# Queries, keys and gates of all four retention heads as one Strassen up stage, passed through HBM

## The chip, the cores and the metric

The kernel is one program on one core of a Trainium2 chip. The metric is the device time of one execution in microseconds (us). The engines are PE (TensorE, matrix products), DVE (VectorE), ACT (ScalarE), POOL (GpSimd) and SP (SyncE, which here only issues DMAs).

## The reference, cut to what matters

A trunk of two layers over 1040 tokens (16 learned ones and 1024 of the input), width 1024. Layer 0 has the "even" mixer (a gated linear recurrence beside latent attention), layer 1 the "odd" mixer (retention). Each mixer is followed by a squared-ReLU MLP of width 4096, and each sublayer ends in a layer norm.

```python
def _odd_mixer(x, pos, w_in, w_out):
    qk = RET_HEADS * RET_QK_DIM                      # 4 heads x 256
    p = x @ w_in
    q, k, v, g = jnp.split(p, [qk, 2 * qk, 2 * qk + RET_MIX], axis=-1)   # RET_MIX = 4 x 512
    q = _rope(q.reshape(B, T, RET_HEADS, RET_QK_DIM), pos)
    k = _rope(k.reshape(B, T, RET_HEADS, RET_QK_DIM), pos) * (RET_QK_DIM ** -0.5)
    ...
    _, o_r = lax.scan(body, s, (to_chunks(q), to_chunks(k), to_chunks(v)))   # retention
    ...
    o = (of * lax.rsqrt(jnp.mean(jnp.square(of), axis=-1, keepdims=True) + EPS)).astype(x.dtype)
    y = o.transpose(0, 2, 1, 3).reshape(B, T, RET_MIX)
    return (jax.nn.silu(g) * y) @ w_out
...
    h = _layernorm(DN_ALPHA * h + mix, ln_mix_g[l], ln_mix_b[l])
    f = jnp.square(jax.nn.relu(h @ mlp_w1[l])) @ mlp_w2[l]
    h = _layernorm(DN_ALPHA * h + f, ln_mlp_g[l], ln_mlp_b[l])
```

## The kernel before

Everything is held transposed: a matrix is 8 tiles of 128 features by the tokens. A number in fp32 is carried as two fp32r parts, hi and lo, which ACT (a cast, L306) and DVE (source minus hi, L353, L634 or L300) make. A product of two such tiles is three matmuls, hi·hi, hi·lo and lo·hi (L333 to L335, in `mm3` and `gemm`).

The SBUF is 50 slots of 128 x 1040 numbers and the PSUM eight banks, handed out in turn. `later` and `pump` run generators in the background of a loop, `queue`, `feed` and `need` do the same for fetching and splitting weights; `advance(pumps, feeds)` calls both. A scheduler then sets the order on each engine, and within an engine the order is kept: an instruction that waits holds all behind it.

The program runs in stages, with their rough place in the profiled execution:

- The even mixer, and its norm: 0 to 500 us.
- The MLP of layer 0, `smlp(0)`: 500 to 1204 us. Its **up** half (`up`, `products`, L768 to L770) is a Strassen scheme: x and the weights are cut into 2 x 2 blocks, seven products of sums take the place of eight. A unit `u` is two times two tiles of weights, 16 units in all; each unit goes over two token halves `q`, with 7 products x 4 tiles x 3 matmuls of 260 columns. ACT (L791) and DVE (L794) collect them out of PSUM, DVE squares (L798), and sums of the result go to HBM (`h_scratch`). The **down** half takes blocks of 4 or 2 such units (`BLOCKS[0] = [4, 4, 4, 2]`) through Strassen again, and the last 4 of the 32 tiles by plain products. The norm (`chunk`, `norm_chunk`) adds squares over features with fp32 matmuls of ones (L524, L558, L570) and here leaves x in SBUF as hi and lo.
- The odd mixer, 1204 to 1925 us, head by head: values `v` (`ret_values`: 8 token tiles x 8 tiles of features x 3 matmuls of 512 columns, then `ret_tail` for the last 16 tokens, L1461 to L1464); keys (`ret_rope`: two tiles in three spans of 348 and 346 columns, the rotation on DVE straight out of PSUM); `ret_turn` (k turned by PE, L1507); queries (two tiles in two spans of 512); for heads 1 to 3 the values stand here, between the turn and the state. Then `retain` (the state, the scores, the output, L1588 to L1590), then the gates (four tiles of 512 columns, Silu on ACT, L1370) with `ret_norm` among them. The gated output of heads 0 to 2 goes to `y_scratch` in HBM through POOL's queue.
- The out projection (end of `odd_mixer`, and `enter`): 1925 to 2120 us. `enter` is the way into a Strassen stage: four norm chunks, x to HBM, and the sums that the seven products need (`sums_of`, `make_x`).
- The MLP of layer 1: as layer 0's, with tokens in quarters of 256, blocks `[4, 4, 4]`, 8 plain tiles at the end and the output: 2120 to 2813 us.

## Time and profile before

| what | us |
|---|---|
| median of three runs | 2818.78 (2817.33 to 2821.24) |
| the profiled execution | 2815.4 |
| its span | 2813.6 |
| PE busy, in 19318 records | 2720.2 (97%) |
| DVE busy | 1741.3 (62%) |
| ACT busy | 1050.1 (37%) |
| POOL busy | 496.8 (18%) |

The span is the time between the first and the last instruction of the profile. An engine's busy time counts overlapping matmuls once. In a window the time that PE is not busy is time lost by the whole program, when PE is the engine that all stages stand on; the granted clock (PEclk, 1.00 is full speed) tells what is lost while it is busy.

### The profile page before, as it was taken

The numbers are of one execution on the slowest core, as the hardware profiler recorded it, in microseconds if no ns is written. First come the engines' busy times: TensorE is split into PE (matmuls) and PEld (weight loads), VectorE is DVE, ScalarE is ACT, GpSimd is POOL, SyncE is SP. The second block draws the span as 40 slices with busy tenths as digits, with TensorE's granted clock in tenths as the row PEclk, the third lists the DMA queues.
The fourth block names the chain that finished last, engine by engine and source line by source line (L and its number), as shares of the span: only waits on it lengthen the run. The fifth ranks groups of instructions, "written<-read, shape, count | busy, mean of one in ns | idle before, by whom it ended". The sixth has DMA issues, their size and how long they took to land. (4 is left out here: it accounts for less than half of the span.)

```text
span 2813.6 us, 46690 instructions
## 1 busy us (share of the span) xinstructions
PE 2720.2 (97%) x19318; PEld 2566.8 (91%) x19318; DVE 1741.3 (62%) x2748; ACT 1050.1 (37%) x1787; POOL 496.8 (18%) x532
## 2 busy tenths in 40 slices
PE   8999999999999999999999999999999999999997
PEld 8898899999999999878878888789999999999997
DVE  6678868755576778544534535354387655677754
ACT  3757744433343233332414224141145333433223
POOL 1024441456520000010000000010004644000010
PEclk9999999999999999999999999999999999999998
DMA  3220130344474235011301313043204444644311
GB/s 137 76 73 5 62 121 31 122 145 155 139 281 145 105 123 167 17 45 50 115 16 45 120 37 114 16 135 128 83 31 136 150 133 153 240 165 145 103 68 60
DMA packets 111941, 294.84 MB, mean 105 GB/s; under 512 B 10529, under 2 KB 46881, under 8 KB 111729
## 3 DMA queue, kind: packets, MB, share of 16 engines
q1 hardware_dynamic: 93168, 225.08, 23.5%
q0 software_dynamic: 17984, 64.65, 6.8%
q8 instruction: 151, 2.47, 0.4%
q10 hardware_dynamic: 576, 2.13, 0.2%
q14 instruction: 62, 0.50, 0.1%
HBM read 206.83 MB, written 81.80 MB: 103 GB/s over the span
## 5 line engine op out<-in xcount | busy, mean ns | idle before, releaser
L768 PE MATMUL p<-s,s 128*128 128x260 f32 (+1 forms) x3248 | 903.1, 284 | 23.3 <-DVE s L893 7.3
L769 PE MATMUL p<-s,s 128*128 128x260 f32 (+1 forms) x3248 | 909.9, 283 | 2.4 <-DVE s L634 2.2
L770 PE MATMUL p<-s,s 128*128 128x260 f32 (+1 forms) x3248 | 895.6, 282 | 5.0 <-DVE s L634 5.0
L333 PE MATMUL p<-s,s 128*128 128x256 f32 (+9 forms) x2614 | 854.7, 329 | 20.8 <-POOL s L381 7.3
L334 PE MATMUL p<-s,s 128*128 128x256 f32 (+9 forms) x2614 | 846.6, 324 | 4.6 <-DVE s L384 2.9
L335 PE MATMUL p<-s,s 128*128 128x256 f32 (+9 forms) x2614 | 843.1, 324 | 5.8 <-DVE s L300 5.8
L306 ACT CAST s<-s 128x1024 fp32r<-128x1024 f32 (+7 forms) x587 | 506.4, 888 | 840.2 <-PE p L770 119.4
L768 PEld LDWEIGHTS p<-s,s 128*128 128x128 f32 x3248 | 607.7, 189 | 30.4 <-ACT s L306 8.8
L769 PEld LDWEIGHTS p<-s,s 128*128 128x128 f32 x3248 | 614.6, 189 | 4.2 <-DVE s L634 3.8
L770 PEld LDWEIGHTS p<-s,s 128*128 128x128 f32 x3248 | 607.6, 189 | 5.7 <-DVE s L634 5.7
L333 PEld LDWEIGHTS p<-s,s 128*128 128x128 f32 (+3 forms) x2614 | 490.8, 188 | 63.5 <-ACT s L1199 10.1
L334 PEld LDWEIGHTS p<-s,s 128*128 128x128 f32 (+3 forms) x2614 | 491.8, 188 | 39.2 <-DVE s L384 3.9
L335 PEld LDWEIGHTS p<-s,s 128*128 128x128 f32 (+3 forms) x2614 | 491.1, 188 | 40.0 <-DVE s L300 6.5
L634 DVE TENSOR_TENSOR s<-s,s 128x1024 fp32r<-128x1024 f32 (+2 forms) x311 | 380.7, 1235 | 108.9 <-ACT s L306 102.9
L791 ACT COPY s<-p 128x260 f32<-128x260 f32 (+1 forms) x256 | 93.5, 373 | 237.5 <-PE p L770 217.3
L893 DVE TENSOR_TENSOR s<-s,p 128x260 f32<-128x260 f32 (+1 forms) x328 | 132.6, 418 | 74.5 <-PE p L770 71.9
L300 DVE TENSOR_TENSOR s<-s,s 128x1024 fp32r<-128x1024 f32 x97 | 118.0, 1224 | 77.8 <-ACT s L306 55.0
L798 DVE SCALAR_TENSOR_TENSOR s<-s 128x1040 f32<-128x1040 f32 (+1 forms) x64 | 83.6, 1306 | 42.1 <-ACT s L791 41.9
L794 DVE TENSOR_TENSOR s<-s,p 128x260 f32<-128x260 f32 (+1 forms) x192 | 78.2, 417 | 44.3 <-PE p L770 35.9
L806 POOL TENSOR_TENSOR s<-s 128x520 f32<-128x520 f32 (+1 forms) x52 | 78.4, 1509 | 133.5 <-DVE s L798 108.6
L1442 DVE TENSOR_TENSOR s<-p,s 128x512 fp32r<-128x512 f32 x32 | 22.0, 690 | 125.4 <-ACT s L1441 125.4
L536 POOL TENSOR_TENSOR s<-s 128x512 f32<-128x512 f32 (+1 forms) x6 | 7.8, 1297 | 479.2 <-DVE s L532 467.6
(212 smaller groups left out, 2611.4 us busy)
## 6 DMA issues: line engine op xcount, KB each, us to landing
s<-in_w SPq DMA_DIRECT2D x76, 512.0 KB, 3.9
s<-h_scratch SPq DMA_DIRECT2D x49, 520.0 KB, 5.9
s<-in_w2s SPq DMA_DIRECT2D x48, 512.0 KB, 4.4
s<-h_scratch SPq DMA_DIRECT2D x42, 512.0 KB, 6.2
h_scratch<-s POOLq DMA_DIRECT2D x28, 520.0 KB, 3.7
y_scratch<-s POOLq DMA_DIRECT2D x24, 512.0 KB, 10.2
s<-y_scratch POOLq DMA_DIRECT2D x24, 512.0 KB, 5.6
h_scratch<-s POOLq DMA_DIRECT2D x24, 512.0 KB, 4.2
```

The lines of the kernel that those rows point to most:

```text
L300: (self.nc.gpsimd if self.pool_lo else self.nc.vector).tensor_sub(lo[:, :n], s[:, :n], hi.f[:, :n])
L306: self.nc.scalar.copy(out, in_)
L333: self.nc.tensor.matmul(ps, wh, xh, start=(i == 0), stop=False)
L334: self.nc.tensor.matmul(ps, wh, xl, start=False, stop=False)
L335: self.nc.tensor.matmul(ps, wl, xh, start=False, stop=(stop and i == n - 1))
L634: (eng or self.nc.vector).tensor_sub(l.t, raw.t, h.f)
L768: nc.tensor.matmul(ps, wh[:, c], xh[:, k, :], start=(start and k == 0), stop=False, skip_group_check=skip)
L769: nc.tensor.matmul(ps, wh[:, c], xl[:, k, :], start=False, stop=False, skip_group_check=skip)
L770: nc.tensor.matmul(ps, wl[:, c], xh[:, k, :], start=False, stop=(k == nk - 1), skip_group_check=skip)
L791: nc.scalar.copy(h[:, {0: 0, 5: 1, 4: 3, 3: 2}[p], :], ps)
L798: nc.vector.scalar_tensor_tensor(h[:, :, :], h[:, :, :], 0.0, h[:, :, :], ALU.max, ALU.mult)
L893: nc.vector.tensor_add(d, d, ps)
```

## The change

The odd mixer's queries, keys and gates of all four heads (32 tiles of 128 output features, 1040 tokens) become a third Strassen up stage (`ODD`), run before the heads: unit 4h is head h's keys, 4h+1 its queries, 4h+2 and 4h+3 its gates. The rotation is done by DVE in SBUF on whole quarters (`rope`), the Silu by ACT, and the results are written by SP's queue to `p_scratch` in HBM, as fp32. The heads then have only the values' products: `ret_load` fetches k and q of a head and splits them, in the background of the values, and `ret_close` does the norm, fetches the gates, multiplies and splits, in the background of the next head's values. `ret_values` now goes through the weights outermost, over two groups of four banks.

For this, x has to come out of layer 0's MLP through `enter`, as at the other entries: blocks `[4, 4, 4]` and 8 plain tiles, the norm in four chunks, x to HBM (`x_odd`) and sums for the seven products. During the last unit of the up stage the eight tiles of x are fetched again and split (`rows`, `fetch_x`, `make_p`), and the values' first weights with them. The out projection takes the residual x from `x_odd` by DMA, where DVE added hi and lo.

```diff
...
-BLOCKS = [[4, 4, 4, 2], [4, 4, 4]]
+BLOCKS = [4, 4, 4]
+ODD = 2
...
-PV = 6
+PV = 2
...
         for h in range(RET):
-            v = [d["wv1"][4 * h + i] for i in range(4)]
-            u += v if h == 0 else []
...
+        self.pairs.append((len(u), len(u) + len(o)))
+        u += o + [d["wv1"][i] for i in range(16)]
...
+            if self.stage == ODD:
+                if u % 4 < 2:
+                    self.later(0, self.rope(h, tabs[i], [self.hd[2 * u + r][:, 2 * n * q:2 * n * q + 2 * n] for r in range(2)]))
+                    return
+                nc.scalar.activation(h[:, :, :], h[:, :, :], AF.Silu)
+                for r in range(2):
+                    nc.sync.dma_start(self.hd[2 * u + r][:, 2 * n * q:2 * n * q + 2 * n], h[:, 2 * r:2 * r + 2, :])
+                self.aside.append(h)
+                return
...
+            if s == 4 and self.stage == ODD:
+                for u, q in streams:
+                    if u % 4 < 2:
+                        t = self.slot(F32, (P, 2, 2 * n))
+                        src = self.d["ropeq"][u // 4] if u % 4 else self.d["ropek"]
+                        nc.sync.dma_start(t[:, :, :], src[:, :, 2 * n * q:2 * n * q + 2 * n].rearrange("c p t -> p c t"))
+                        tabs.append(t)
...
+        self.queue(("X", s))
+        if s:
+            self.queue(("p", s - 1))
+        if s == 6:
+            self.queue(("X", 7), ("p", 6), ("p", 7), *[("v", i) for i in range(4)])
...
         for u in range(2, 16):
-            self.queue(("w", u + 1))
-            self.up([(u, 0), (u, 1)], True, at=moves(0) if u == 15 else None, rates=(0, 4 if u == 15 else 1), nxt=True)
+            if more or u < 15:
+                self.queue(("w", u + 1))
+            self.up([(u, 0), (u, 1)], True, at=at if u == 15 else None, rates=(0 if more else 2, 4 if u == 15 else 1), nxt=more or u < 14)
...
+        rec, wr = [self.ops["r", i] for i in range(4)], []
+        self.queue(*[("R", i) for i in range(4, 8)])
...
+        ws, y = [self.weight(reserve=50) for _ in range(4)], [self.ops["r", i] for i in range(4, 8)]
...
-        for c in range(4):
-            def gemm(ps, m):
-                self.gemm(ps, ws[m // 2], h, c * n, c * n + n, k0=4 * (m % 2))
...
-            tmp = self.chunk(c, gemm, True, rates=(5, 0))
...
-        return x, [t for ts in self.acc for t in ts]
+            self.enter(rec, wr, y, ws, self.g11, self.b11, out=self.out)
+        else:
+            self.layer(ODD)
+            self.enter(rec, wr, y, ws, self.g01, self.b01)
...
+        pr, xo = self.hd, self.xd
+        self.up_stage(self.rows)
+        x = []
+        for k in range(KT):
+            self.need("p", k)
+            x.append(self.ops["r", k])
...
+            kf, k, q = [], [], []
+            self.later(0, self.ret_load(pr, 8 * h, 0, T, k, kf))
+            self.later(0, self.ret_load(pr, 8 * h + 2, META, SEQ, q))
+            v = self.ret_values(x, h == 0)
+            if h == RET - 1:
+                for t in x:
+                    self.drop(*t)
+            self.settle()
             kt = self.ret_turn(h, kf)
-            cq, sq = self.slot(F32, (P, SEQ)), self.slot(F32, (P, SEQ))
-            nc.sync.dma_start(cq[:, :], d["ropeq"][h, 0])
-            nc.sync.dma_start(sq[:, :], d["ropeq"][h, 1])
...
-            if h:
-                v = self.ret_values(x)
             o = self.retain(h, q, k, v, kt)
...
-            for m in range(4):
...
-                    ps = self.bank("b")[:, :hi - lo]
-                    self.gemm(ps, w, x, META + lo, META + hi)
-                    silu = nc.scalar.activation(sg[m][:, lo:hi], ps, AF.Silu)
...
-                if m == NORM_AT:
-                    self.ret_norm(o, onesr)
...
+            self.later(0, self.ret_close(pr, h, o, ys))
+        y = self.reload(0) + self.reload(1)
...
-                nc.vector.tensor_add(self.acc[c][k // 4][:, k % 4, :], xh.f[:, cols], xl.f[:, cols])
...
+        self.acc = [self.x_chunk(c, xo, META) for c in range(4)]
...
             for c in range(4):
                 self.part(c, mp, lambda ps, m: self.gemm(ps, w[m % 2], y, c * n, c * n + n), True)
+                self.advance(6, 0)
             self.drop(*w[0], *w[1])
+            if mp == 1:
+                self.settle()
+                self.drop(aux, self.vc)
+                rec = self.reload(2)
...
+    def ret_load(self, pr, i, off, n, out, keep=None):
+        for j in range(2):
+            f = self.slot(F32, (P, n))
+            self.nc.sync.dma_start(f[:, :], pr[i + j][:, off:off + n])
+            yield True
+            h, l = self.slot(F32R, (P, n)), self.slot(F32R, (P, n))
+            self.split(f[:, :], h[:, :], l[:, :], h.f)
+            out.append((h, l))
+            if keep is None:
+                self.drop(f)
+            else:
+                keep.append(f)
+            yield True
+
+    def rope(self, h, tab, dst):
+        nc, n = self.nc, 2 * self.qn
+        t = self.slot(F32, (P, 2, n))
+        a, b = (h.t.rearrange("p (j r) n -> p j (r n)", j=2)[:, j, :] for j in range(2))
+        nc.vector.tensor_mul(t[:, :, :], a.unsqueeze(1).broadcast_to((P, 2, n)), tab[:, :, :])
+        yield True
+        nc.vector.tensor_mul(a, b, tab[:, 1, :])
+        yield True
+        nc.vector.tensor_mul(b, b, tab[:, 0, :])
+        yield True
+        nc.vector.tensor_sub(t[:, 0, :], t[:, 0, :], a)
+        yield True
+        nc.vector.tensor_add(t[:, 1, :], t[:, 1, :], b)
+        for r in range(2):
+            nc.sync.dma_start(dst[r], t[:, r, :])
+        self.drop(h, tab, t)
+        yield True
+
...
+    def ret_close(self, pr, h, o, ys):
...
+        yield from self.ret_norm(o)
+        for m in range(4):
+            g = self.slot(F32, (P, SEQ))
+            nc.sync.dma_start(g[:, :], pr[8 * h + 4 + m][:, META:])
+            nc.vector.tensor_mul(g[:, :], g[:, :], o[m][:, :])
+            self.drop(o[m])
+            yield True
+            yh, yl = self.slot(F32R, (P, SEQ)), self.slot(F32R, (P, SEQ))
+            self.split(g[:, :], yh[:, :], yl[:, :], yh.f)
...
+            if h < RET - 1:
+                for e, t in enumerate((yh, yl)):
+                    nc.gpsimd.dma_start(self.scratch[4 * h + m, e], t[:, :])
...
-        for i, (lo, hi) in enumerate(ATOK):
-            n = hi - lo
-            self.settle(hi)
...
-            self.pump(PV)
+        for group in (range(0, 4), range(4, 8)):
+            ps = [self.bank("all") for _ in group]
+            for u in range(4):
+                for i, t in zip(group, ps):
...
+                    for k in (2 * u, 2 * u + 1):
...
+                        nc.tensor.matmul(t, xh, wh, start=(k == 0), stop=False)
+                        nc.tensor.matmul(t, xh, wl, start=False, stop=False)
+                        nc.tensor.matmul(t, xl, wh, start=False, stop=(k == KT - 1))
...
+                    self.pump(PV)
+        self.ret_tail(x, ws, first)
...
+        if h < RET - 1:
+            self.ahead(4, 1, 1)
...
```

How the order on the engines moves is shown at three places. Names: `p_` is a PSUM tile, `s_` an SBUF slot, with a number of its own for each use; a row reads engine line, operation, out<-moving,stationary operand, shape.

**PE, from a head's turn of k to the products behind it.** Before, head 1: the last product of the keys, the turn (L1507), the queries' products (x is `s_1645`, `s_1646`).

```order
L335 MATMUL p_2179_17277<-s_1659_12684,s_2148_17039 128x346
L1507 MATMUL p_2184_17340<-consts_116,s_2161_17137 128x128
L1507 MATMUL p_2184_17340<-consts_116,s_2162_17138 128x128
L1507 MATMUL p_2185_17345<-consts_116,s_2161_17137 128x128
L1507 MATMUL p_2185_17345<-consts_116,s_2162_17138 128x128
L333 MATMUL p_2200_17380<-s_1645_12670,s_2163_17139 128x512
L334 MATMUL p_2200_17380<-s_1646_12671,s_2163_17139 128x512
```

After, head 1: the last product of the values' tail, then the turn (L1528; `s_2142` is the fetched k0, `s_2145` the fetched k1) and the scores of `retain` (`s_2149`, `s_2150` are hi and lo of q0, `s_2152`, `s_2153` of q1, `s_2143`, `s_2144` of k0, `s_2146`, `s_2147` of k1).

```order
L1508 MATMUL p_2158_17876<-s_2110_17552,s_2013_16885 48x512
L1528 MATMUL p_2162_17901<-consts_116,s_2142_17703 128x128
L1528 MATMUL p_2163_17906<-consts_116,s_2142_17703 128x128
L333 MATMUL p_2185_18005<-s_2149_17739,s_2143_17705 128x144
L333 MATMUL p_2188_18023<-s_2149_17739,s_2143_17705 128x272
L334 MATMUL p_2185_18005<-s_2150_17740,s_2143_17705 128x144
L335 MATMUL p_2185_18005<-s_2149_17739,s_2144_17706 128x144
L334 MATMUL p_2188_18023<-s_2150_17740,s_2143_17705 128x272
L335 MATMUL p_2188_18023<-s_2149_17739,s_2144_17706 128x272
L1528 MATMUL p_2162_17901<-consts_116,s_2145_17715 128x128
L1528 MATMUL p_2163_17906<-consts_116,s_2145_17715 128x128
L333 MATMUL p_2185_18005<-s_2152_17753,s_2146_17717 128x144
```

The queries' and the values' products, which stood between the turn and the scores, no longer stand there.

**DVE, at the same place of head 1.** Before: the last values' lo parts (L1442), the tail (L1467, L1470), the state's lo parts (L1522) and the scores' (L1560).

```order
L1442 TENSOR_TENSOR s_2066_16257<-p_2073_16423,s_2062_16253 128x512
L1442 TENSOR_TENSOR s_2066_16257<-p_2074_16450,s_2062_16253 128x512
L1467 TENSOR_TENSOR s_2076_16494<-p_2075_16477,s_2076_16494 16x512
L1470 TENSOR_TENSOR s_1700_13284<-s_2076_16494,s_1700_13284 16x512
L1522 TENSOR_TENSOR s_2078_16501<-p_2079_16502,s_2077_16500 128x512
L1522 TENSOR_TENSOR s_2078_16501<-p_2080_16517,s_2077_16500 128x512
L1560 SCALAR_TENSOR_TENSOR s_2087_16544<-p_2085_16536,consts_116 128x112
L1560 SCALAR_TENSOR_TENSOR s_2097_16602<-p_2095_16594,consts_116 128x128
```

After: the last values' lo parts (L1487) and the tail (L1513, L1516) with the lo parts of q0, q1 and k1 (L353) among and behind them, then the turned k (L1531).

```order
L1487 TENSOR_TENSOR s_2119_17563<-p_2156_17767,s_2115_17559 128x512
L1487 TENSOR_TENSOR s_2119_17563<-p_2157_17768,s_2115_17559 128x512
L1513 TENSOR_TENSOR s_2159_17893<-p_2158_17876,s_2159_17893 16x512
L353 TENSOR_TENSOR s_2150_17740<-s_2148_17729,s_2149_17739 128x1024
L353 TENSOR_TENSOR s_2153_17754<-s_2151_17743,s_2152_17753 128x1024
L1516 TENSOR_TENSOR s_2014_16886<-s_2159_17893,s_2014_16886 16x512
L353 TENSOR_TENSOR s_2147_17718<-s_2145_17715,s_2146_17717 128x1040
L1531 SCALAR_TENSOR_TENSOR s_2161_17900<-p_2162_17901,consts_116,s_2160_17899 128x256
L1531 SCALAR_TENSOR_TENSOR s_2161_17900<-p_2163_17906,consts_116,s_2160_17899 128x256
```

Three lo parts of 128 x 1024 or 1040 elements now stand between the values' tail and the turned keys.

**PE, from the last head's retention to what follows.** Before: the last products of `retain` (L1588 to L1590), then the gates' products (`p_2288`); the norm's matmuls of ones (L1618) stand 96 rows further down.

```order
L1589 MATMUL p_2260_17953<-s_2268_18041,s_2214_17516 128x512
L1590 MATMUL p_2260_17953<-s_2268_18041,s_2218_17520 128x512
L334 MATMUL p_2288_18111<-s_1648_12673,s_2278_18092 128x512
L335 MATMUL p_2288_18111<-s_1647_12672,s_2279_18093 128x512
L333 MATMUL p_2288_18111<-s_1649_12674,s_2278_18092 128x512
```

After: the last products of `retain` (L1611 to L1613), then the out projection's (`p_2457`).

```order
L1612 MATMUL p_2408_19512<-s_2416_19600,s_2326_18960 128x512
L1613 MATMUL p_2408_19512<-s_2416_19600,s_2330_18964 128x512
L333 MATMUL p_2457_19712<-s_2418_19635,s_2446_19691 128x256
L334 MATMUL p_2457_19712<-s_2419_19636,s_2446_19691 128x256
L335 MATMUL p_2457_19712<-s_2418_19635,s_2447_19692 128x256
```

And 50 rows further down the last head's norm (L1645, L1646) among the out projection's products.

```order
L335 MATMUL p_2456_19711<-s_2432_19663,s_2444_19686 128x256
L1645 MATMUL p_2461_19773<-s_2462_19774,s_2013_16885 128x512
L335 MATMUL p_2464_19787<-s_2418_19635,s_2444_19686 128x256
L333 MATMUL p_2464_19787<-s_2420_19639,s_2443_19685 128x256
L334 MATMUL p_2464_19787<-s_2421_19640,s_2443_19685 128x256
L335 MATMUL p_2464_19787<-s_2420_19639,s_2444_19686 128x256
```

The out projection's products now follow the last retention directly, and the norm stands among them, after 50 matmuls of 256 columns where it stood after 96 of 512.

## Rows read from the trace of the kernel before

**Rows 1.** The page's first part: busy us, share of the span, instructions

```profile
PE 2720.2 (97%) x19318; PEld 2566.8 (91%) x19318; DVE 1741.3 (62%) x2748; ACT 1050.1 (37%) x1787; POOL 496.8 (18%) x532
```

**Rows 2.** Windows: bounds, length; busy (count) per engine; PEclk; DMA share; GB/s

```profile
680.00:780.00 100.00, 100.00 (x837) 100.00 (x836) 57.38 (x69) 32.51 (x60) 54.72 (x50) 1.00 0.45 147
1590.00:1640.00 50.00, 50.00 (x217) 40.42 (x216) 15.87 (x25) 6.91 (x12) 1.83 (x3) 1.00 0.06 21
1265.00:1275.00 10.00, 10.00 (x65) 10.00 (x65) 5.19 (x12) 1.83 (x4) 0.00 (x0) 1.00 0.10 30
1600.00:1620.00 20.00, 20.00 (x87) 16.18 (x87) 6.36 (x10) 2.40 (x4) 0.00 (x0) 1.00 0.07 30
```

**Rows 3.** The chain that ended last: start, us, engine, line, instructions

```profile
2091.59 0.86 PE p L524 x4
```

**Rows 4.** Windows, as in rows 2: where PE idles on work the change touches

```profile
1080.00:1100.00 20.00, 18.08 (x141) 17.22 (x142) 17.72 (x46) 6.34 (x12) 0.00 (x0) 1.00 0.47 161
1100.00:1120.00 20.00, 19.29 (x161) 19.11 (x161) 16.14 (x33) 6.22 (x6) 0.00 (x0) 1.00 0.45 145
1180.00:1200.00 20.00, 15.62 (x78) 13.48 (x77) 16.02 (x29) 13.13 (x30) 2.68 (x2) 0.83 0.33 107
1240.00:1260.00 20.00, 14.15 (x59) 11.45 (x58) 7.91 (x9) 5.89 (x8) 0.00 (x0) 0.83 0.25 79
1920.00:1940.00 20.00, 18.26 (x152) 17.88 (x152) 13.09 (x29) 4.19 (x4) 4.24 (x8) 1.00 0.81 289
```

**Rows 5.** PE's timeline: start, us, instruction, idle before it and releaser

```profile
1185.82 3.83 PE L524 MATMUL p<-s,consts 128*128 128x260 f32 x8 [4.38 <-DVE s L532]
1252.69 0.66 PE L335 MATMUL p<-s,s 128*128 128x348 f32 x1 [5.85 <-DVE s L300]
```

**Rows 6.** Windows, as in rows 2: places like those that the change adds

```profile
2680.00:2700.00 20.00, 15.71 (x118) 15.01 (x117) 15.14 (x19) 7.96 (x8) 0.00 (x0) 0.91 0.40 140
500.00:520.00 20.00, 17.54 (x133) 16.47 (x132) 15.07 (x20) 14.48 (x27) 3.01 (x4) 1.00 0.30 106
2180.00:2200.00 20.00, 17.06 (x132) 16.66 (x132) 13.93 (x14) 6.14 (x10) 13.41 (x11) 0.93 0.44 145
580.00:600.00 20.00, 18.92 (x156) 18.51 (x155) 10.60 (x14) 6.07 (x12) 11.20 (x11) 1.00 0.46 147
820.00:840.00 20.00, 16.18 (x129) 15.37 (x127) 16.02 (x19) 10.51 (x12) 0.00 (x0) 1.00 1.06 379
2440.00:2460.00 20.00, 16.17 (x115) 15.67 (x114) 16.51 (x24) 7.25 (x9) 0.00 (x0) 0.83 0.65 224
```

**Rows 7.** ACT's instructions by shape: busy us, mean ns, idle before them

```profile
L306 ACT CAST s<-s 128x1024 fp32r<-128x1024 f32 x330 | 340.5, 1049 | 509.5 <-PE p L769 70.2 <-DVE s L661 67.6 <-PE p L770 63.1
L1466 ACT COPY s<-p 16x512 f32<-16x512 f32 x4 | 2.3, 576 | 11.0 <-PE p L1462 11.0
```

**Rows 8.** DVE's instructions by shape: busy us, mean ns, idle before them

```profile
L353 DVE TENSOR_TENSOR s<-s,s 128x1040 fp32r<-128x1040 f32 x4 | 5.0, 1242 | 5.3 <-ACT s L306 5.2
L353 DVE TENSOR_TENSOR s<-s,s 128x1024 fp32r<-128x1024 f32 x4 | 4.9, 1226 | 5.0 <-ACT s L306 5.0
L1467 DVE TENSOR_TENSOR s<-p,s 16x512 f32<-16x512 f32 x4 | 2.7, 679 | 10.0 <-ACT s L1466 10.0
L1510 DVE SCALAR_TENSOR_TENSOR s<-p,consts,s 128x256 fp32r<-128x256 f32 x16 | 7.2, 477 | 12.7 <-ACT s L1509 12.7
L798 DVE SCALAR_TENSOR_TENSOR s<-s 128x1040 f32<-128x1040 f32 x32 | 41.6, 1301 | 15.6 <-ACT s L791 15.5
L576 DVE TENSOR_TENSOR s<-s,s 128x1040 f32<-128x1040 f32 x16 | 19.1, 1236 | 0.2
L661 DVE TENSOR_TENSOR s<-s,s 128x512 f32<-128x512 f32 x56 | 40.2, 720 | 0.8 <-DMA s<-in_w 0.2
```

**Rows 9.** DMA issues: queue, count, KB of one, median us to landing

```profile
s<-in_w SPq DMA_DIRECT2D x76, 512.0 KB, 3.9
y_scratch<-s POOLq DMA_DIRECT2D x24, 512.0 KB, 10.2
```

More of the change, by code (lines that the diff above doesn't have):

```diff
@@ new lines, in rows, with fetch_x, make_p @@
+    def rows(self, s, p):
+        self.queue(("X", s))
+        if s:
+            self.queue(("p", s - 1))
+        if s == 6:
+            self.queue(("X", 7), ("p", 6), ("p", 7), *[("v", i) for i in range(4)])
+    def fetch_x(self, k):
+        raws = []
+        yield from self.take(1, raws, F32, (P, T))
+        self.nc.sync.dma_start(raws[0].t, self.xd[k])
+        self.ops["raw", k] = raws[0]
+        yield True
+    def make_p(self, k):
+        got = []
+        yield from self.pieces(self.ops["raw", k], got, (P, T))
+        self.ops["r", k] = got
@@ L871, in smlp @@
                 self.queue(("W", u + 2))
[L872 removed]
+            if u == end - 2:
                 self.queue(*[("R", i) for i in range(4)])
[L874 to L876 removed]
                 self.queue(*[x for i in range(4) for x in (("v", i), ("r", i))])
```

258 lines of the change are left out of this document (95 added, 163 removed).

## Prediction

> **What bounds the kernel now.** The page's first part comes first: PE is busy 2720.2 of 2813.6 us, 97%, DVE 62%, ACT 37% [rows 1]. PE takes its instructions in order, so a time comes out of two sums: how long PE needs for its matmuls, and how long it waits between them. The windows give both. Where the supply is good, a window is full: 100.00 of 100 us with 837 matmuls of 260 columns in layer 0's up stage, 50.00 of 50 with 217 matmuls of 512 columns in the values, 10.00 of 10 with 65 of 346 or 348 columns in the keys [rows 2]. Such a window also gives the price of a matmul. A record's own duration does not: matmuls overlap there, so length by count is what counts. The other thing to see is that waits sit at the joints between stages, while the heads of the odd mixer, which are to be changed, are full: 20.00 of 20 us [rows 2].
>
> **Part 1, PE's work.** By the order of both kernels PE gets 2736 more matmuls of 260 columns: the new up stage has 16 units x 2 halves x 7 products x 4 tiles x 3 = 2688, the dropped block of two units took 336, and four plain tiles more in layer 0 bring 384. It loses 1152 of 512 columns (4 heads x 6 tiles x 2 spans x 24) and 576 of 346 or 348 (4 heads x 2 tiles x 3 spans x 24). Of the fp32 matmuls of ones in the norms, 16 of L524 go and 4 of L558 come, each two records.
>
> A window's count can be off by one or two matmuls cut at its edges, so a price lies between 100/837 and 100/835: 0.1195 to 0.1198, I take 0.11965; 50/217 to 50/215: 0.2304 to 0.2326, 0.2315; 10/65 to 10/63: 0.1538 to 0.1587, 0.15625 [rows 2]. Four L524 records take 0.86 us, so one matmul of ones 0.43 [rows 3]. The sum: 2736 x 0.11965 = +327.4; 1152 x 0.2315 = -266.7; 576 x 0.15625 = -90.0; 12 x 0.43 = -5.2. **Together -34.5 us**, between -32 and -37 by the bounds.
>
> **Part 2, waits that go.** 1080 to 1120 is the dropped block: 1.92 + 0.71 idle. 1180 to 1200 is the layer norm at the end of layer 0, where PE waits 4.38 us for DVE's L532 and then runs at a clock of 0.83 for the window (0.17 x 20 = 3.4 us more). 1240 to 1260 is head 0's first keys, which wait 5.85 us for a weight's lo part (L300), again with 0.83. 1920 to 1940 is the out projection's start, 1.74 idle [rows 4, 5]. **Together -21.4 us.** All of that code is removed or rewritten; what comes in its place is the next part.
>
> **Part 3, waits that come.** No trace shows them, so each is priced by the nearest place.
> - *Layer 0's last plain tiles and norm*: now built like layer 1's end, where 2680 to 2700 has 4.29 idle and a clock of 0.91 (1.8). I take 6; 1.7 if it goes like 1920, 7.8 if like 1180 [rows 4, 6].
> - *Start of the up stage behind `enter`*: 500 to 520 (2.46) and 2180 to 2200 (2.94, and 0.93 x 20: 1.4) are the two entries that exist. I take 5; 2.5 to 7 [rows 6].
> - *Units 2 to 15*: one window in the present stage has 1.08 idle, others none [rows 2, 6]. The new load is the rotation: instead of one squaring of 1.30 us a unit's half needs a multiplication over 1040 elements (1.24) and four operations over 520 (0.72 each), 4.1 us [rows 8]. DVE is busy 57.38% of a unit of 168 x 0.11965 = 20.1 us, 11.5 us; with two halves it is 11.5 - 2.6 + 8.2 = 17.1 of 20.1 in the eight units of keys and queries. That is work with cover: PE waits only where the collecting additions out of PSUM stand behind it. ACT gets one Silu where it is 33% busy: nothing. SP gets the writes to HBM, each waiting for the last addition of its rotation, and behind them the raw weights of the unit after next, which land 3.9 us after issue [rows 9] and have a unit of cover: nothing, and 3 to 4 us a unit if the cover is gone. I take 4; 0 to 9 (1.08 in each such unit).
> - *Up stage to values*: in the last unit eight rows of x, four weights of the values, the last gates' writes and head 0's k and q move, 20 x 0.52 MB, some 10 MB. At 379 GB/s, the most that the table shows [rows 6], that is 27 us against a unit of 20. The joints with such traffic cost 3.82 (820 to 840) and 3.83 with a clock of 0.83 (2440 to 2460: 7.2 together). I take 7; 3.8 to 11.
> - *Head 0*: its loads stand in the background of the values with nothing before them. I take 2; 0 to 4.
> - *Heads 1 to 3, values to scores*: this is the largest. Behind the tail of the values PE's order has the turn of k and the scores at once, which need hi and lo of q0, q1 and k1. ACT's order has the tail's copy (0.58 us) and then q0's cast (1.05) [rows 7]; DVE's has the tail's addition (0.68), lo of q0 (1.23), of q1 (1.23), the tail's second part (0.68), lo of k1 (1.24) and two turned tiles (2 x 0.48) [rows 8]. In a line that is 7.65 us from the tail to the state; about 20 small matmuls of at most 0.12 fill 2.4 of them. So 5.3 idle, and the clock behind it 0.91 or 0.83 for a window, 1.8 to 3.4: 8 a head, **24 in all**. The low end is 5 a head (full clock), the high end 11 (nothing filled, and 0.83). Before, the queries' products, and for these heads the values', stood between the turn and the state and hid the same work.
> - *Last head to the out projection*: the norm now has 50 matmuls of 256 columns ahead of it (about 6 us at the price for 260) where 96 of 512 (22 us) hid it, and the first weights' casts stand behind its squares on ACT. The nearest are 2440 to 2460, 7.2, which I take; 1.7 (as 1920) to 9.2 (as 1240, 5.85 + 3.4) [rows 4, 6].
>
> Background work in the values (split of k and q, `ret_close`) is at nothing: DVE is busy 15.87 and ACT 6.91 of 50 us there [rows 2]. If that cover were gone it would add to the heads' line above.
>
> Together 6 + 5 + 4 + 7 + 2 + 24 + 7 = **+55 us**.
>
> **The sum.** 2815.4 - 34.5 - 21.4 + 55 = 2814.5 for a profiled execution. The median of the runs was 3.4 us above the profiled one, so 2817.9, and I say **2818**: no change that can be measured. (0.2% of this kernel, 5.6 us, is about what a measurement can tell from none.)
>
> **The rivals.**
> - *The waits are hidden: 2797.* The scheduler puts work where it is ready, and a wait that is short leaves the clock at full speed, as the 1.74 at 1920 did [rows 4]. With 3 instead of 8 us in heads 1 to 3 (-15), and 6 less over the other joints, 2818 - 21 = 2797. Against it: the three windows in the rows with more than 4 us idle (1180, 1240, 2680) all show 0.83 or 0.91 [rows 4, 6].
> - *The heads wait for their fetches: 2836.* Place: heads 1 to 3, slots. The fetches of q0 and k1 take slots that the previous head's writes to `y_scratch` hold until they land, 10.2 us after issue [rows 9]. If they are given free less than about 10 us before the tail ends, the fetch itself (3.9 us or more) and the cast behind it come into the line: some 6 more a head, and 2818 + 18 = 2836. For it: eight such writes a head now fall into the next head's values, 8 x 24 x 0.2315 = 44 us, with the fetches. Against it: DMA is at 0.06 there [rows 2].
> - *DVE bounds the up stage: 2838.* 17.1 of 20.1 us leaves 3; weight sums that POOL doesn't take would have to come to more. Over 23 us a unit, 8 x 3 = 24 less the 4 taken.
> - *Narrow matmuls cost as much as wider ones: 2915.* More matmuls, each with a weight load: PEld is full, 100.00 of 100, at 260 columns and 40.42 of 50 at 512 [rows 2]. If the load set the pace, a 260 would cost what a 346 does, 0.156: 2736 x 0.0366 = +100. The counts say no: 0.1197 against 0.2315 is 0.460 and 0.452 ns a column, so the load hides nearly whole. The Trainium skill (TensorE: Matmul & The Clock Gate, "Back-to-back issue gap") says that in a stream of weight loads and matmuls both set the spacing, with 81 ns at 128 columns and 131 at 512, so that two narrow matmuls would cost well above one wide one; an estimate by that ratio (98 ns at 260 columns, 0.75 of a wide one) would have the change lose over 100 us. The trace disagrees on both durations and their ratio.
>
> That the change doesn't do what it says is out: the order shows the counts above.
>
> **How the numbers follow.** My forecast has 0.50; its own spread, by the bounds of part 3, is about 2803 to 2832, of which 0.27 lies within 0.2% of before, 0.12 below, 0.11 above. Waits hidden 0.28, late fetches 0.17, DVE 0.04, narrow matmuls 0.01. Faster 0.12 + 0.28 = 0.40; the same 0.27; slower 0.11 + 0.22 = 0.33. The range goes from 2797 to the late fetches with a little on either side, 2796 to 2840.
>
> **What would show it.** In the profile after, PE should have some 34 us less work (busy time falls by that and by the clock lost in part 2), 260-column windows at 835 to 837 a 100 us, and the heads' joints 5 to 6 us idle each with a clock under 1.00, released by DVE's L353. If these joints are released by DMA from `p_scratch`, the second rival holds; if they show under 2 us at full clock, the first. DVE above 95% in windows of keys' and queries' units would speak for the third, fewer than 800 matmuls in 100 full us for the fourth. The prediction would be wrong above all by the 24 us of the heads' line, which is read off an order and durations, not off a wait that was ever seen.

## The result, and the profile after

The changed kernel takes 2838.73 us (median of four runs, 2831.98 to 2841.49) against 2818.67 us (2817.33 to 2821.24). The ratio is 1.0067, with a 95% interval of 1.0048 to 1.0086: **slower by 0.7%, 20 us**, where no measurable change was forecast. The time lies within the stated range (2796 to 2840), close to the 2836 of the second rival and to the 2838 of the third; as a number it can't tell the two apart, the windows below do. The profiled execution took 2831.98 us, 16.6 more than the profiled one of before; it is the quickest of the four, and the others are 6.5 to 9.5 us above it.

The page's first part of the changed kernel, as [rows 1]:

```profile
PE 2705.3 (96%) x20302; PEld 2592.9 (92%) x20302; DVE 1825.4 (64%) x2710; ACT 1099.6 (39%) x1850; POOL 528.3 (19%) x548
```

PE is busy 15 us less and the span is 17 us longer: PE now stands idle for 124.9 us of the span, where it was 93.4. Windows of the changed kernel at the places that the prediction priced (columns as in [rows 2]):

```profile
1300.00:1400.00 100.00, 100.00 (x837) 100.00 (x836) 60.91 (x87) 35.74 (x63) 13.69 (x9) 1.00 0.37 128
1060.00:1080.00 20.00, 17.59 (x145) 17.18 (x144) 12.99 (x18) 9.33 (x10) 0.00 (x0) 1.00 0.72 255
1080.00:1100.00 20.00, 16.13 (x110) 15.40 (x109) 11.67 (x15) 3.38 (x4) 0.00 (x0) 0.83 0.33 118
1200.00:1220.00 20.00, 18.75 (x146) 17.76 (x144) 13.95 (x19) 13.89 (x26) 3.01 (x4) 1.00 0.37 125
1220.00:1240.00 20.00, 15.80 (x110) 14.98 (x111) 17.99 (x24) 7.13 (x12) 0.00 (x0) 0.91 0.41 132
1260.00:1280.00 20.00, 19.32 (x158) 18.91 (x158) 13.91 (x20) 9.29 (x15) 7.77 (x4) 1.00 0.31 107
1520.00:1540.00 20.00, 15.11 (x88) 12.53 (x87) 8.27 (x10) 9.58 (x14) 4.89 (x17) 1.00 0.66 229
1580.00:1600.00 20.00, 17.72 (x96) 13.66 (x94) 9.85 (x25) 8.29 (x21) 0.00 (x0) 0.91 0.03 10
1660.00:1680.00 20.00, 15.15 (x64) 10.53 (x62) 12.74 (x15) 9.56 (x14) 5.31 (x9) 0.90 0.89 313
1680.00:1700.00 20.00, 17.54 (x81) 14.14 (x80) 8.40 (x25) 5.75 (x17) 0.00 (x0) 0.76 0.02 8
1760.00:1780.00 20.00, 16.05 (x66) 11.61 (x65) 12.22 (x15) 8.20 (x13) 3.88 (x7) 0.88 0.84 296
1780.00:1800.00 20.00, 17.31 (x87) 14.44 (x86) 8.13 (x23) 6.07 (x17) 0.00 (x0) 0.78 0.00 1
1860.00:1880.00 20.00, 15.15 (x67) 10.15 (x66) 11.98 (x19) 9.67 (x18) 5.94 (x11) 0.85 0.90 313
1900.00:1920.00 20.00, 16.29 (x91) 14.18 (x90) 8.04 (x14) 8.67 (x14) 0.00 (x0) 0.96 1.06 378
1920.00:1940.00 20.00, 20.00 (x147) 19.82 (x147) 16.02 (x20) 4.52 (x5) 0.00 (x0) 0.87 0.26 87
```

The first of them is the new up stage, full, with 837 matmuls, as [rows 2] has it for the old one: DVE is at 60.91 of 100 us there, and in no window of 20 us from 1280 to 1500 above 16.2, so the third rival (DVE bounds the up stage) is out. All others are joints (1240 to 1260, with 0.14 idle, is not counted). An idle time is the window's length less PE's busy time; the clock's share is (1 - PEclk) times that busy time, an estimate, since PEclk is a mean over the window. Put against the prediction's terms, on the two profiled executions:

| term | predicted | measured |
|---|---|---|
| PE's work | -34.5 | -29 (busy time corrected for the clock) |
| waits that go [rows 4] | -21.4 | -19.7 |
| end of layer 0 (1060 to 1100) | 6 | 9.0 |
| start of the up stage (1200 to 1280) | 5 | 7.6 |
| units 2 to 15 (1280 to 1520) | 4 | 0 (no window with over 0.3 idle) |
| up stage to values (1520) | 7 | 4.9 |
| head 0 (1580) | 2 | 3.9 |
| heads 1 to 3 (1660 to 1700, 1760 to 1800, 1860 to 1900) | 24 | 33.4 |
| last head to the out projection (1900 to 1940) | 7 | 7.0 |
| the rest | 0 | about 0 |
| sum | -1 | +16.6 |

Half of the new waits, 33 us, is at one kind of place: between the values of heads 1 to 3 and their scores. PE's timeline there in head 1 (start, us, instruction, idle before and releaser):

```profile
1675.50 0.50 PE L333 MATMUL p<-s,s 128*128 128x144 f32 x2 [3.74 <-ACT s L306]
1676.76 0.49 PE L334 MATMUL p<-s,s 128*128 128x144 f32 x1 [0.76 <-DVE s L353]
1683.98 0.79 PE L333 MATMUL p<-s,s 128*128 128x512 f32 x1 [2.26 <-DVE s L1531]
```

ACT's at the same place:

```profile
1672.85 1.04 ACT L306 CAST s<-s 128x1024 fp32r<-128x1024 f32 x1 [4.41 <-DMA s<-p_scratch]
1673.92 0.58 ACT L1512 COPY s<-p 16x512 f32<-16x512 f32 x1
1674.40 1.04 ACT L306 CAST s<-s 128x1024 fp32r<-128x1024 f32 x1
```

SP's queue, first what it issues (start, us, line), then its waits at gates, k and q from 1640 to 1690 (us in total, times, longest):

```profile
1656.07 7.89 SPq L1411 DMA_DIRECT2D s<-p_scratch  x3
1669.21 1.14 SPq L1411 DMA_DIRECT2D s<-p_scratch  x1
```

```profile
SPq L1445 <- DVE s L395: 21.2, 1, 21.2
SPq L1411 <- DMA y_scratch<-s: 6.0, 1, 6.0
SPq L1411 <- DVE s L1446: 5.3, 1, 5.3
```

The scores wait 3.74 us for the second of these casts, that of q0: it ends at 1675.44, and PE starts at 1675.50. It stands on ACT behind the tail's copy (L1512) and behind the cast of q1, which waits 4.41 us for the DMA out of `p_scratch`.

That DMA is late for two reasons. SP issues the four fetches of k and q (L1411) only from 1656 to 1670 us: its queue had stood 21.2 us at the last of the previous head's gates (L1445, until the norm's L395 was done), then 5.3 us for the gating (L1446) and 6.0 us for a write to `y_scratch` to land, which holds the slot. And the fetch of q1, issued at 1662.88, takes 9.9 us to land, where that of k0, issued at 1656.07, took 3.4: from 1657 to 1667 the eight writes of the gated output are issued, and the DMA share is 0.89 from 1660 to 1680.

The values had begun at 1626. Head 2 has the same wait (3.31 us); in head 3 it shows as 3.43 us for the tail's addition (L1513), whose copy stands behind q1's cast. These are the waits of the second rival. The lo parts that the forecast counted (L353) add 0.76, and the turned keys (L1531) 2.26.

### The profile page after: what moved, and what is told of

Same layout as the page of the kernel before. It is cut to its first block, busy times and chain, and to the rows that moved or that the text cites. A ratio compares the mean times of both kernels' runs of the same rounds, so it can differ in the third digit from the quotient of the medians.

```text
span 2830.2 us, 49069 instructions
## 1 busy us (share of the span) xinstructions
PE 2705.3 (96%) x20302; PEld 2592.9 (92%) x20302; DVE 1825.4 (64%) x2710; ACT 1099.6 (39%) x1850; POOL 528.3 (19%) x548
## 5 line engine op out<-in xcount | busy, mean ns | idle before, releaser
L763 PE MATMUL p<-s,s 128*128 128x260 f32 (+1 forms) x4032 | 1121.6, 285 | 35.9 <-ACT s L786 10.7
L764 PE MATMUL p<-s,s 128*128 128x260 f32 (+1 forms) x4032 | 1131.3, 283 | 5.5 <-DVE s L629 5.5
L765 PE MATMUL p<-s,s 128*128 128x260 f32 (+1 forms) x4032 | 1113.4, 283 | 1.2 <-DVE s L629 1.2
L306 ACT CAST s<-s 128x1024 fp32r<-128x1024 f32 (+5 forms) x586 | 546.1, 948 | 834.0 <-PE p L765 123.1
L763 PEld LDWEIGHTS p<-s,s 128*128 128x128 f32 x4032 | 754.9, 189 | 46.2 <-ACT s L786 14.1
L764 PEld LDWEIGHTS p<-s,s 128*128 128x128 f32 x4032 | 764.4, 190 | 7.2 <-DVE s L629 6.5
L765 PEld LDWEIGHTS p<-s,s 128*128 128x128 f32 x4032 | 755.2, 190 | 1.6 <-DVE s L629 1.6
L333 PE MATMUL p<-s,s 128*128 128x256 f32 (+9 forms) x1910 | 581.8, 307 | 36.6 <-ACT s L306 10.1
L334 PE MATMUL p<-s,s 128*128 128x256 f32 (+9 forms) x1910 | 575.1, 302 | 8.3 <-DVE s L629 4.2
L335 PE MATMUL p<-s,s 128*128 128x256 f32 (+9 forms) x1910 | 572.2, 301 | 1.5 <-DVE s L300 1.0
L629 DVE TENSOR_TENSOR s<-s,s 128x1024 fp32r<-128x1024 f32 (+1 forms) x366 | 458.7, 1264 | 116.6 <-ACT s L306 105.1
L333 PEld LDWEIGHTS p<-s,s 128*128 128x128 f32 (+2 forms) x1910 | 361.6, 190 | 54.5 <-ACT s L306 11.5
L334 PEld LDWEIGHTS p<-s,s 128*128 128x128 f32 (+2 forms) x1910 | 363.5, 190 | 16.9 <-DVE s L629 4.7
L335 PEld LDWEIGHTS p<-s,s 128*128 128x128 f32 (+2 forms) x1910 | 362.4, 190 | 8.4 <-DVE s L300 1.3
L786 ACT COPY s<-p 128x260 f32<-128x260 f32 (+1 forms) x384 | 140.7, 373 | 358.8 <-PE p L765 336.7
L536 POOL TENSOR_TENSOR s<-s 128x520 f32<-128x520 f32 (+1 forms) x8 | 10.3, 1294 | 815.1 <-DVE s L532 804.0
L654 DVE TENSOR_TENSOR s<-s 128x512 f32<-128x512 f32 x72 | 53.0, 736 | 119.2 <-DMA h_scratch<-s 45.9
L1481 PE MATMUL p<-s,s 128*128 128x512 f32 x256 | 99.5, 394 | 1.6 <-ACT s L306 1.6
```

The source lines that it names most:

```text
L306: self.nc.scalar.copy(out, in_)
L333: self.nc.tensor.matmul(ps, wh, xh, start=(i == 0), stop=False)
L334: self.nc.tensor.matmul(ps, wh, xl, start=False, stop=False)
L335: self.nc.tensor.matmul(ps, wl, xh, start=False, stop=(stop and i == n - 1))
L629: (eng or self.nc.vector).tensor_sub(l.t, raw.t, h.f)
L763: nc.tensor.matmul(ps, wh[:, c], xh[:, k, :], start=(start and k == 0), stop=False, skip_group_check=skip)
```

## The experiments

**1. Fetch early.** The four fetches of a head's k and q go into the background queue behind the previous head's norm and ahead of its gating; their splits stay behind it.

```diff
-            self.later(0, self.ret_load(pr, 8 * h, 0, T, k, kf))
-            self.later(0, self.ret_load(pr, 8 * h + 2, META, SEQ, q))
+            raws = []
+            self.later(0, self.ret_fetch(pr, 8 * h, raws))
+            if h:
+                self.later(0, self.ret_close(pr, h - 1, o, ys))
+            self.later(0, self.ret_load(raws, 0, T, k, kf))
+            self.later(0, self.ret_load(raws, 2, SEQ, q))
...
-            self.later(0, self.ret_close(pr, h, o, ys))
+            self.later(0, self.ret_norm(o))
```

> The changed kernel, with one thing moved: the fetches of a head's k and q out of HBM (four DMAs) are queued behind the previous head's norm and ahead of its gating, so that they need no slot that a write of the gated output still holds; their splits stay behind the gating. Theory A (at heads 1 to 3 PE waits because the fetches come late: SP waits 6.0 us for a y_scratch write there and ACT 4.41 us for the DMA of q): the waits of 3.3 to 3.7 us on the cast at 1675, 1774 and 1872 us go, with a part of the clock lost behind them; 8 us a head of the 11 seen, 2839 - 24 = 2815 median (2810 to 2822). Theory B (the line of casts and lo parts behind the values' tail costs the time, whenever the data lands): those waits stay at 3 us and more, 2834 to 2842.

Measured: 2808.04 us (2806.76 to 2809.69), a ratio to before of 0.9955 (0.9940 to 0.9970). That is 30.7 us less than the changed kernel, and now faster than before (the kernel before has 2818.67 us beside the changed kernel, 2821.24 beside runs 1 to 4 and 2820.4 to 2820.5 beside the others, so a difference between two of these groups is good to 2 or 3 us). SP's queue, ACT at the joint of head 1, and the windows at the heads' joints (the last window is that of the last head and the out projection):

```profile
1612.04 2.02 SPq L1417 DMA_DIRECT2D s<-p_scratch  x4
```

```profile
1668.35 1.05 ACT L306 CAST s<-s 128x1024 fp32r<-128x1024 f32 x1
1672.93 0.58 ACT L1522 COPY s<-p 16x512 f32<-16x512 f32 x1 [3.04 <-PE p L1518]
```

```profile
1660.00:1680.00 20.00, 18.82 (x91) 14.05 (x90) 16.24 (x20) 12.15 (x19) 5.77 (x10) 1.00 0.83 286
1760.00:1780.00 20.00, 19.04 (x114) 15.73 (x113) 11.46 (x28) 8.59 (x22) 0.00 (x0) 1.00 0.18 66
1840.00:1860.00 20.00, 19.13 (x98) 14.05 (x97) 13.35 (x24) 9.66 (x21) 7.72 (x14) 1.00 0.98 324
1880.00:1900.00 20.00, 15.84 (x93) 14.60 (x93) 11.22 (x11) 10.02 (x11) 0.00 (x0) 0.83 0.74 262
```

All four fetches are issued at 1612, 44 us earlier, and the three joints lose 1.4, 1.0 and 1.3 us (1.2 at 1660 and 0.2 behind it, 0.9 at 1840 and 0.4 behind it) with the clock at 1.00: 3.6 us where 33.4 were. As many casts and lo parts are made as in the changed kernel. Theory A holds, with more than it promised; that the line of casts costs the time whenever the data lands is out. With the data there early, the order on ACT is another as well: the last cast of k and q begins at 1668.35, ahead of the tail's copy at 1672.93, where in the changed kernel the casts stood around that copy and behind it. So two things go together here, data that is there and casts that no longer stand at the tail; no run parts them.

**2. Fetch and split early.** Both the fetches and the splits stand ahead of the gating.

```diff
             self.later(0, self.ret_load(pr, 8 * h + 2, META, SEQ, q))
+            if h:
+                self.later(0, self.ret_close(pr, h - 1, o, ys))
...
-            self.later(0, self.ret_close(pr, h, o, ys))
+            self.later(0, self.ret_norm(o))
```

> The changed kernel, with fetch and split of k and q both ahead of the previous head's gating in the background queue; the gating's casts and lo parts now stand last ahead of the values' tail. Theory A (late fetches): like the kernel with the fetches alone moved, 2815, within 4 us of it. Theory B (the line of casts behind the tail): this kernel gains and that one doesn't: 2815 here against 2834 or more there. Theory C (any work in the background has to end by the head's joint, so what is moved ahead pushes the gating into the joint): 2830 or more, with waits of the scores on the tail's additions behind the gating's lo parts.

Measured: 2851.26 us (2848.10 to 2852.43), ratio 1.0106 (1.0091 to 1.0121). Theory C: the wait has only changed its owner. PE's timeline in head 1, DVE's, and SP's waits from 1510 to 1700:

```profile
1692.51 0.60 PE L333 MATMUL p<-s,s 128*128 128x272 f32 x1 [13.91 <-DVE s L1515]
```

```profile
1680.85 1.22 DVE L1448 TENSOR_TENSOR s<-s,s 128x1024 f32<-128x1024 f32 x1 [1.17 <-DMA s<-p_scratch]
1688.30 1.23 DVE L1448 TENSOR_TENSOR s<-s,s 128x1024 f32<-128x1024 f32 x1 [3.83 <-DMA s<-p_scratch]
1690.63 1.23 DVE L353 TENSOR_TENSOR s<-s,s 128x1024 fp32r<-128x1024 f32 x1 [1.11 <-ACT s L306]
1691.78 0.67 DVE L1515 TENSOR_TENSOR s<-p,s 16x512 f32<-16x512 f32 x1
```

```profile
SPq L1447 <- DMA y_scratch<-s: 5.9, 1, 5.9
SPq L279 <- DMA y_scratch<-s: 11.5, 1, 11.5
```

With k's and q's parts in ten slots, the gates of the previous head are fetched one by one into slots that a write to `y_scratch` gives free (SP waits 5.9 us for such a write at a gate's fetch, L1447, and 11.5 at a weight's, L279, in the same queue). Each gating (L1448) waits for its fetch, 1.2 to 3.8 us, and the tail's addition (L1515) stands behind the last of them on DVE: PE waits 13.91 us. So the fetch has to be early here; the split, which takes six more slots than the fetches, had better wait.

**3. The turn of k earlier.** As 2, and k is turned between the two groups of the values' products.

```diff
-            kt = self.ret_turn(h, kf)
+            kt = kts[0]
...
         for group in (range(0, 4), range(4, 8)):
+            if group[0]:
+                self.settle()
+                mid()
```

> As the kernel with fetch and split of k and q first, and the turn of k put between the two groups of the values' products, so that the state at the joint needs no turned tile that is made behind the tail. Theory A with a rest of its own at the joint (2.3 to 2.7 us for DVE's turned tiles, L1531, at 1684 and 1783 us, and the clock at 0.50 behind it): 3 to 4 us a head less than the kernel without this, 2815 - 14 = 2801 (2796 to 2812). If the wait on the turned tile was only a follow-up of the late fetch: the same as the kernel without this, within 3 us.

Measured: 2851.07 us (2848.08 to 2856.18), as 2. The joint of head 1 is no better: PE is idle for 14.7 us from 1660 to 1700, and for 14.6 in run 2. It stands on a kernel whose joints wait for something else, so it says only that the turn isn't what ends last there, as the second expectation had it. For the kernel of run 1 this was not tried.

**4. The end of layer 0 alone.** The kernel before, with blocks `[4, 4, 4]` and 8 plain tiles.

```diff
-BLOCKS = [[4, 4, 4, 2], [4, 4, 4]]
+BLOCKS = [[4, 4, 4], [4, 4, 4]]
```

> The kernel before with one part of the change alone: layer 0's MLP goes through Strassen's down half in three blocks of four units, and 8 tiles instead of 4 by plain products; the norm, and all of the odd mixer, stay as before. PE gets 384 - 336 = 48 matmuls of 260 columns more, 5.7 us. Theory A (the waits at the end of layer 0 come from enter and the new norm, not from the dropped block): 2819 + 6 = 2825, with the 2.6 us of waits at 1080 to 1120 replaced by some of the same size. Rival (the dropped block is itself a loss, as the waits of 2.4 and 3.9 us with a clock of 0.83 at 1060 to 1100 of the changed kernel suggest): 2831 to 2834.

Measured: 2819.38 us (2813.93 to 2820.22) against 2821.24, ratio 0.9991 (0.9982 to 1.0001). The 5.7 us of 48 matmuls more don't show in these medians; the two profiled executions differ by 4.6 us in span. Windows of the joint and of the norm:

```profile
1060.00:1080.00 20.00, 18.45 (x155) 18.24 (x153) 12.34 (x18) 10.22 (x11) 0.00 (x0) 1.00 0.75 262
1080.00:1100.00 20.00, 14.26 (x92) 13.38 (x93) 15.01 (x19) 6.39 (x7) 0.00 (x0) 0.83 0.39 127
1180.00:1200.00 20.00, 20.00 (x140) 18.93 (x139) 15.78 (x21) 11.06 (x22) 5.21 (x2) 1.00 0.08 22
```

The joint (1060 to 1100) loses 9.7 us, as the changed kernel's 9.0, where [rows 4] have 2.6 for the dropped block; but the norm, which lost 7.0 us at 1180 [rows 4], is full here. So the two kinds of waits balance, this part of the change is worth about nothing in the time (where the 5.7 us of matmuls went stays open), and neither theory's number is right: the waits that the rival saw are there, and another goes for them.

**5 to 7. The last head, and the last unit.** Run 5: the out projection's first weights are fetched and split during the last retention. Run 6: two of the values' weights are queued among the rows of x, not behind them. Run 7: both. All three on the kernel of run 1.

```diff
+VA, VB = 2, 4
...
+        if s in (VA, VB):
+            self.queue(("v", 0 if s == VA else 1))
         if s == 6:
-            self.queue(("X", 7), ("p", 6), ("p", 7), *[("v", i) for i in range(4)])
+            self.queue(("X", 7), ("p", 6), ("p", 7), *[("v", i) for i in range(2, 4)])
...
-        if h < RET - 1:
-            self.ahead(4, 1, 1)
+        self.ahead(4, 1, 1) if h < RET - 1 else self.ahead(4, 2, 2)
```

> As the kernel with the early fetches (2808.0), and in the last head's retention the next weights (the out projection's first two) are fetched and split ahead, as the other heads do. Theory A (PE waits 3.7 us at 1891 us, and loses 2.7 to the clock behind it, because that weight is fetched only at 1879 and cast at 1890, behind the squares of the last norm): 2808 - 5 = 2803 (2800 to 2805). Rival (the reloaded y or the norm ends last there): 2806 to 2810, with another releaser of the same wait.

> As the kernel with the early fetches (2808.0), and in the last unit of the up stage the values' first two weights are fetched and split among the rows of x, not behind all eight. Theory A (the 2.6 us on the cast of the first weight, whose slot a write to p_scratch held until 1528 us, are a matter of order): 2808 - 4 = 2804 (2802 to 2806). Rival (the last unit moves 10 MB at 300 to 430 GB/s, and what isn't late in one place is late in another): 2806 to 2811, with the waits moved to the rows of x or to the collecting additions.

> The kernel with the early fetches and both moves, weights ahead at the last head and the values' first weights among the rows of x. If both theories hold and the gains add up: 2808 - 9 = 2799. If neither: 2808.

Measured: 2803.52 (2802.88 to 2807.61), 2804.81 (2800.02 to 2805.41) and 2795.89 us (2794.40 to 2797.36). Both moves do what theory A says of them: 4.5 and 3.2 us alone. Together they give 12.2, more than the sum. By the windows each empties its joint, of 6.9 us (run 5, at 1880) and 6.2 (run 6, at 1520), 13.1 in all. What can hide this is the start of the program, 0 to 480 us, which no edit touches: idle and clock together are 35.6 us there in the profiled execution of run 1, 38.4 in run 5, 41.8 in run 6, 33.4 in run 7. The idle time is 31 to 33 us in all four; the rest is the clock. The two joints in the kernel with both are full at full clock, where run 1 has 4.16 idle and 0.83 at 1880:

```profile
1520.00:1540.00 20.00, 20.00 (x127) 18.04 (x126) 12.29 (x13) 12.31 (x17) 7.95 (x18) 1.00 0.69 244
1880.00:1900.00 20.00, 20.00 (x150) 19.34 (x150) 10.21 (x12) 7.20 (x8) 0.53 (x1) 1.00 0.76 267
```

Run 7's ratio to before is 0.9909 (0.9895 to 0.9924): **0.9% faster than before, 43 us less than the changed kernel**, with the same products.

**8. The rotation.** On the kernel of run 1, four of the rotation's five operations are left out.

> As the kernel with the early fetches (2808.0); of the rotation of keys and queries in the up stage only one multiplication by the cosines is left, on all four tiles at once, and the four other operations of each half unit are left out: 4 x 0.72 us of DVE less, 5.8 us in each of eight units. Theory A (DVE has room, 17 of 20 us a unit, and no window between 1280 and 1520 us shows PE idle): 2806 to 2809. Rival (DVE's load in the up stage costs time that shows elsewhere, at the joint behind the last unit or in collecting additions): 8 units x 1 us, 2800 or less.

Measured: 2796.10 us (2793.78 to 2800.81), 11.9 less than run 1. Theory A is wrong in its result, and the rival's number (2800 or less) holds. Windows without the rotation, then of run 1:

```profile
1300.00:1400.00 100.00, 100.00 (x836) 100.00 (x835) 48.76 (x62) 35.61 (x64) 16.70 (x11) 1.00 0.40 139
1200.00:1220.00 20.00, 19.93 (x161) 19.34 (x160) 15.38 (x22) 13.93 (x27) 2.26 (x3) 1.00 0.15 54
1220.00:1240.00 20.00, 18.23 (x146) 17.40 (x145) 16.82 (x20) 10.09 (x17) 0.75 (x1) 1.00 0.53 187
1260.00:1280.00 20.00, 20.00 (x169) 20.00 (x168) 9.08 (x11) 9.86 (x16) 4.22 (x3) 1.00 0.36 131
1520.00:1540.00 20.00, 18.86 (x98) 15.93 (x98) 11.10 (x12) 9.89 (x12) 3.79 (x6) 1.00 0.74 278
```

```profile
1200.00:1220.00 20.00, 18.14 (x141) 17.14 (x139) 13.94 (x20) 14.34 (x26) 3.01 (x4) 1.00 0.40 133
1220.00:1240.00 20.00, 16.41 (x116) 15.59 (x117) 18.11 (x25) 6.49 (x12) 0.00 (x0) 0.91 0.41 137
1260.00:1280.00 20.00, 18.97 (x156) 18.56 (x155) 13.82 (x20) 9.15 (x15) 5.98 (x4) 1.00 0.31 107
1520.00:1540.00 20.00, 15.17 (x83) 13.19 (x82) 9.09 (x11) 11.15 (x15) 4.93 (x17) 0.91 0.87 305
```

In the middle of the stage theory A is right: PE is full at 1300 with 836 matmuls, DVE at 49% here and 60.89 of 100 us in run 1. The gain is at the two ends. At the start (1200 to 1280) the lost time falls from 8.0 to 1.8 us, and at the joint to the values (1520) from 6.2 to 1.1. At the end no rotation is running any more, since the last two units are gates; that slots and queue make the difference there is argued, not shown. ACT's timeline of run 1 has the cast of the values' first weight waiting for the landing of a write to `p_scratch`:

```profile
1528.09 2.18 ACT L306 CAST s<-s 128x1024 fp32r<-128x1024 f32 x2 [5.94 <-DMA p_scratch<-s]
```

**9 and 10. Other units first.** On the kernel of run 7, the first two units are gates (run 9), and in run 10 also the keys and queries of all heads follow at once, and gates come last.

```diff
+PAIRS = [2, 3, 0, 1, 4, 5, 6, 7, 8, 9, 10, 11, 12, 13, 14, 15]
...
+        o = [o[2 * i + r] for i in PAIRS for r in range(2)]
...
             if self.stage == ODD:
+                u = PAIRS[u]
```

> As the kernel with the early fetches and both moves (2795.9), and the first two units of the up stage, which run while DVE still makes the sums of x and of the weights, compute head 0's gates instead of its keys and queries; these come as units 2 and 3. Theory A (without most of the rotation the stage's start loses 6 us less, 1.8 instead of 8.0 between 1200 and 1280 us, because DVE is full there: 9.7 of 10 us): 2796 - 6 = 2790 (2787 to 2792). Rival (the start is bound by the sums of x alone, and what the kernel without rotation gained there was slots): 2794 to 2798.

> As the kernel with gates in the first two units, and all heads' keys and queries in units 2 to 9, the other gates in units 10 to 15, so that no rotation stands near the end of the stage. Theory A (the rotation costs at the two ends of the stage, and the end is covered already by the values' weights fetched first): 2790, within 3 us of the kernel with only the first units exchanged. Rival (the rotation's slots and writes still cost at the joint to the values): 2786 or less. Rival (eight units of rotation in a row leave DVE no time to catch up, at 17 of 20 us a unit): 2794 or more.

Measured: 2796.30 (2789.52 to 2797.11) and 2795.04 us (2789.78 to 2800.07); against 2795.89 of run 7 neither is a difference. The gains of theory A are not there; the numbers of its rivals are met, but not their causes: in run 10 PE is full from 1300 to 1400 with DVE at 80.02 of 100 us. In the traces (that of run 9 is its quickest execution, 2789.52) the start is better, as windows of run 9 and then of run 7 show:

```profile
1200.00:1240.00 40.00, 36.29 (x277) 35.09 (x277) 31.30 (x40) 26.63 (x45) 3.01 (x4) 0.96 0.36 122
1240.00:1280.00 40.00, 40.00 (x335) 40.00 (x335) 23.89 (x35) 16.04 (x27) 7.42 (x4) 1.00 0.44 150
```

```profile
1200.00:1240.00 40.00, 36.01 (x273) 34.59 (x272) 31.93 (x41) 22.92 (x41) 3.01 (x4) 0.96 0.28 95
1240.00:1280.00 40.00, 37.23 (x301) 36.20 (x301) 32.22 (x44) 15.32 (x25) 7.66 (x5) 1.00 0.41 145
```

From 1240 to 1280 DVE has 24 us of work instead of 32 and PE is full, 2.8 us better, but the first part of the start is as it was. Of the 6 us that run 8 gained there, about 3 are the rotation's place; what the rest is stays open. The start of the program can hide the 2.8 in the medians too: from 0 to 480 us the profiled executions of runs 7, 9 and 10 lose 33.4, 37.2 and 42.2 us.

## Why the prediction was wrong

- **PE's work, -34.5: near.** PE has 984 records more, as counted (2736 - 1728 - 24), and the price holds to the matmul, 837 in 100 us in the new stage. Busy time corrected for the clock gives -29, outside the bounds of -32 to -37 (the prices as stated give -31.5 to -37.6); the 5 to 6 us between are not assigned to a place. The rival of narrow matmuls is out by its own sign, which wanted fewer than 800 in a full window: the price of 0.1195 us at 260 columns against 0.2315 at 512 stays. The Trainium skill (TensorE: Matmul & The Clock Gate, "Back-to-back issue gap"), which stands beside that rival, has 81 ns at 128 columns and 131 at 512. The traces disagree: 231.5 ns at 512 columns in the kernel before, 119.5 at 260 in both.
- **Waits that go, -21.4: right** (19.7).
- **Heads 1 to 3, 24: the step that failed.** The place was right, the cause was not, and the size was short by 9.4 us: the largest single miss in the 20.7 us between 2818 and 2838.7. The forecast took the order of ACT and DVE behind the tail and added up durations, as if the data lay there; it also left out that q1's cast stands ahead of the tail's copy on ACT, so that one late fetch holds back both. And it gave the late fetch, the second rival, 0.17 on the ground that DMA is at 0.06 in the values [rows 2]. That share was read where no gated output was being written, and a share says nothing on when a fetch may begin. In the changed kernel the fetches began behind the previous head's gating and the landing of a write ([rows 9] had that row, 10.2 us; the wait here is 6.0), and then shared the DMA engines with these writes, at 0.89. Run 1 moves the fetches alone, and gives back 30.7 us, more than the 20.1 that the change had cost.
- **The second rival: right in its cause, lucky in its number.** Its 2836 is the forecast and 18 us more at these heads; they had 9.4 more, and the other 11.3 of the 20.7 us come from other terms.
- Of the 9.4 us that the term was short, the idle time has 3.4 (19.3 instead of 15.9), and the clock has the rest: 14.1 instead of 8. Two waits a joint, 3.74 and 2.26 us in head 1, came with a lower clock over two windows (0.90 and 0.76; in head 3 0.85 and 0.98), where the forecast took one at 0.83 or 0.91.
- **The up stage, 4 + 5 + 7: 12.5 together, but for another reason.** Inside it the cover that was named, three free microseconds of DVE a unit, held: nothing was lost. At its ends, leaving out most of the rotation gave back 11.9 us (run 8), but moving it away from both ends gave nothing in the median (run 10, with the joint at 1520 already emptied by run 6's move); how much is the rotation and how much slots and queue stays open. DVE is full only at the start, 9.72 of 10 us from 1220 to 1230. The forecast's row of waits inside the old stage was short by one (1.13 us from 600 to 620 before).
- **End of layer 0 and last head: near** (9.0 for 6, 7.0 for 7), and the last was a matter of when a weight is fetched (run 5). Head 0 lost 3.9 for 2; no run was made on it.
- **The median.** Three of four runs are 6.5 to 9.5 us above the profiled one; the forecast added 3.4, taken from before. Where these runs lost it can't be seen from a profile of the quickest; that one lost 32.6 us from 0 to 480, at full clock throughout, where the profiled one of before lost 37.6.
